# Fourteen gate tiles of a hybrid encoder block: full products, or seven block products to a pair of tiles

## The chip, the core and the metric

The kernel runs on one core of a Trainium2 chip. A core has TensorE (PE, matrix products; its weight loads are listed apart as PEld), VectorE (DVE), ScalarE (ACT), GpSimdE (POOL) and SyncE (SP), which here only issues transfers between DRAM and SBUF, the on-chip memory. PE writes to PSUM, eight banks of 128 x 512 float32. The engines run side by side, each through its own instructions in order; semaphores tie them together. The metric is the device time of one execution in microseconds (us); the kernel before takes 1192.48 us, the median of three runs (1191.15 to 1193.78).

## The reference

One layer on x of 1024 positions x 1024 channels, all float32:

```
xn = RMSNorm(x) * g
u, z_a, v, b, c, z_b, g_a, g_b = split(xn @ W_in)          # eight units of 1024 columns
y  = D*u + S5 scan forward + S5 scan backward              # 64 groups of 16 channels, state 64
y  = gelu(y);  y = y * sigmoid(y @ w_glu);  y_a = y * silu(z_a)
y_b = b * conv3(c * v) * silu(z_b)
merged = sigmoid(g_a) * (y_a @ w_branch_a) + sigmoid(g_b) * (y_b @ w_branch_b)
out = RMSNorm(x + merged @ w_out) * final_g
```

## The kernel before

**Layout.** Channels stand on the 128 partitions, positions along the free axis. A tile is 128 channels x 1024 positions, so 1024 channels are K = 8 tiles. Every float32 operand of a product is split in two: `hi` (the value cast to fp32r, by ACT, L808 or L115) and `lo` (the rest, by DVE, L809 or L116). One output tile of a product is 48 matmuls of 128x128 weights with 512 moving columns: 8 input tiles x 3 (hi·hi, hi·lo, lo·hi) x 2 halves of the positions (`matmuls`, L125 to L138).

**Order of the work.** After the norm and the first four tiles of u come 52 output tiles of W_in, one after the other (`projections`, the list `items`, L774 to L786): four of u, 32 for the convolution branch, eight of z_a, eight of g_b (unit 7; `gb` takes the sigmoid and stores it to DRAM, `gbd`). Between them, placed by an estimate of PE's and DVE's time (`est`, `vec`), stands the S5 layer: `ssm`, run by `beside`. In this stretch the order on PE and DVE is the one the code is written in (`manual_schedule`); on ACT and SP, and on all engines afterwards, a scheduler sets it before the program runs. When `ssm` is through, its memory is given back, the pool `p2` takes it (L822), and the eight tiles of y_b are loaded from DRAM and split there (L823 to L831).

**Then** come four products with eight output tiles each: `ob` (y_b with w_branch_b; each tile times its gate `gbd` gives `m1`), `ga` (unit 6, the gate g_a; `sga` in SBUF), `glu` and `oa`; last `o`, the product with w_out, 17 groups of 24 matmuls. While `ob` and `ga` run, ACT and DVE work out gelu (`yt`, `yq`, `yg`, L873 to L887), tile by tile, from pieces that SP loads (`yt<-yd`, eight transfers to a tile).

**Buffers.** `t4` is a ring of five 128x1024 tiles for whatever is short-lived; weights have two buffers each for `wraw`, `whi` and `wlo`; PSUM has two double-bank tiles (`mm`) for output tiles and four single banks (`bg`) for the rest.

## Time and profile before

| | |
|---|---|
| median of the runs | 1192.48 us |
| the profiled execution, its own time | 1191.38 us |
| its span, first to last instruction | 1189.6 us |
| PE busy | 1157.0 us, 97% |
| DVE busy | 682.8 us, 57% |
| ACT busy | 422.6 us, 36% |
| mean granted TensorE clock | 0.997 of full speed |

The profiled execution lies 1.1 us under the median, and 1.8 us of its time lie outside the span. PE's matmuls overlap, so one matmul's duration (389 ns) is longer than the step from one to the next; the step is a stretch's time over its count. The same holds in part for DVE, whose next instruction starts a little before the one ahead has ended.

### The profile page before, as it was taken

Reading aid. Unit: us, or ns where it says so; the run is one execution under the profiler, and the core shown is the slowest. Engines: PE = TensorE matmul, PEld = TensorE weight load, DVE = VectorE, ACT = ScalarE, POOL = GpSimd, SP = SyncE. Lnnn points to the kernel's source line nnn. Section 1 sums busy time; section 2 is a strip of 40 time slices with the busy share of each in tenths; the row PEclk is TensorE's granted clock in tenths of the full one; section 3 lists DMA queues with packets and bytes.
Section 4 is the critical chain, followed back from the end, with each engine's and each line's share of the span. In section 5 each row is a group of like instructions: output and inputs, shape, how many; then the busy total and the mean of one; then the engine's idle time right before and its main releaser. Section 6 shows DMA issues by size and latency. Waiting matters only on the chain.

```text
span 1189.6 us, 14821 instructions
## 1 busy us (share of the span) xinstructions
PE 1157.0 (97%) x5926; PEld 960.2 (81%) x5926; DVE 682.8 (57%) x1081; ACT 422.6 (36%) x482; POOL 14.5 (1%) x59
## 2 busy tenths in 40 slices
PE   6999999998899999999999999999999999999997
PEld 4778888877788888888888888888888888887886
DVE  6854698884889869868853311323614235446234
ACT  6344742456215561451363311211414114124111
...
GB/s 283 74 149 284 245 180 70 65 117 194 108 71 63 154 143 71 69 97 118 81 137 208 164 141 166 135 36 76 137 54 36 106 106 67 40 53 270 14 36 106
DMA packets 157817, 140.53 MB, mean 118 GB/s; under 512 B 10892, under 2 KB 138036, under 8 KB 157620
## 3 DMA queue, kind: packets, MB, share of 16 engines
...
HBM read 106.00 MB, written 29.36 MB: 114 GB/s over the span
## 4 chain that ended last, share of the span: by engine, by line
PE 91%; DVE 3%; ACT 2%; issue 2%; DMA 1%; POOL 0%; POOLq 0%; SPq 0%; ACTq 0%; DVEq 0%
PE ps_p L132 46%; PE ps_glu L132 7%; PE ps_ga L132 7%; PE ps_ob L132 7%; PE o L952 7%; PE ps_oa L132 7%; PE xps_x L552 2%; PE ps_u L132 2%; PE yps_y L582 1%; PE yps_y L581 1%; PE yps_y L580 1%; PE kf_y L631 1%; DMA wor<-in_w_out_dram 0%; POOL r_x L145 0%; DMA x<-in_x_dram 0%
## 5 line engine op out<-in xcount | busy, mean ns | idle before, releaser
L132 PE MATMUL ps_p<-xnh,wh_p 128*128 128x512 f32 x832 | 260.6, 394 | 0.0
L132 PE MATMUL ps_p<-xnl,wh_p 128*128 128x512 f32 x832 | 256.6, 390 | 0.0
L132 PE MATMUL ps_p<-xnh,wl_p 128*128 128x512 f32 x832 | 256.3, 389 | 0.0
L132 PEld LDWEIGHTS ps_p<-xnl,wh_p 128*128 128x128 f32 x832 | 156.2, 188 | 33.0
L132 PEld LDWEIGHTS ps_p<-xnh,wl_p 128*128 128x128 f32 x832 | 156.2, 188 | 32.9
L132 PEld LDWEIGHTS ps_p<-xnh,wh_p 128*128 128x128 f32 x832 | 153.3, 188 | 32.6 <-issue 3.2
L115 ACT CAST wh_p<-wr_p 128x1024 fp32r<-128x1024 f32 x52 | 54.7, 1052 | 227.6 <-PE ps_p L132 151.1
L116 DVE TENSOR_TENSOR wl_p<-wr_p,wh_p 128x1024 fp32r<-128x1024 f32 x52 | 63.4, 1218 | 77.7 <-ACT wh_p L115 77.7
L668 DVE TENSOR_TENSOR SB<-SB,st 128x32 f32<-128x32 f32 (+2 forms) x232 | 98.7, 425 | 8.0
L664 DVE TENSOR_TENSOR st<-SB,ac 128x64 f32<-128x64 f32 (+2 forms) x116 | 80.0, 690 | 8.1 <-DMA ac<-acd 5.2
L952 PE MATMUL o<-wo,mh 128*128 128x512 f32 (+1 forms) x272 | 79.8, 377 | 0.8 <-ACT mh L808 0.8
L952 PEld LDWEIGHTS o<-wo,mh 128*128 128x128 f32 x272 | 50.0, 188 | 10.5 <-ACT mh L808 1.2
L952 PE MATMUL o<-wo,ml 128*128 128x512 f32 (+1 forms) x136 | 51.3, 377 | 0.3 <-DVE ml L809 0.3
L540 DVE TENSOR_TENSOR g_x<-bdt_x,pwt_x 128x1024 f32<-128x1024 f32 x16 | 19.6, 1223 | 45.9 <-DMA bdt_x<-bd 27.6
L555 ACT COPY SB<-xps_x 64x512 f32<-64x512 f32 x32 | 35.2, 1101 | 21.5 <-PE xps_x L552 21.1
L610 ACT COPY Sx_y<-SB 64x1016 f32<-64x1016 f32 x16 | 33.9, 2122 | 22.1 <-DVE SB L668 21.8
L552 PE MATMUL xps_x<-U_x,bdt_x 128*128 128x128 f32 x256 | 33.0, 285 | 8.4 <-DVE bdt_x L542 4.4
L116 DVE TENSOR_TENSOR wl_glu<-wr_glu,wh_glu 128x1024 fp32r<-128x1024 f32 x8 | 9.8, 1224 | 54.3 <-ACT wh_glu L115 54.3
L552 PEld LDWEIGHTS xps_x<-U_x,bdt_x 128*128 128x128 f32 x256 | 32.0, 200 | 10.4 <-issue 9.7
L862 DVE TENSOR_TENSOR m<-ps_ob,m 128x1024 f32<-128x1024 f32 x8 | 9.8, 1224 | 51.7 <-PE ps_ob L132 51.6
L132 PE MATMUL ps_ob<-ybl,wh_ob 128*128 128x512 f32 x128 | 39.4, 389 | 0.0
L132 PE MATMUL ps_ob<-ybh,wl_ob 128*128 128x512 f32 x128 | 39.4, 389 | 0.0
...
## 6 DMA issues: line engine op xcount, KB each, us to landing
...
```

Of the source, the lines that this page charges most:

```text
L115: S.copy(out=hi, in_=raw)
L116: V.tensor_tensor(out=lo, in0=raw, in1=hi.bitcast(F32), op=ALU.subtract)
L132: nc.tensor.matmul(out=ps[:, 512 * h:512 * h + 512], lhsT=l[:, k, :], rhs=r[k][:, 512 * h:512 * h + 512], start=(k == 0 and i == 0), stop= ...
L540: V.tensor_tensor(out=g_, in0=Wi, in1=er, op=ALU.mult)
L552: nc.tensor.matmul(out=xps[:, P * j:P * j + P], lhsT=Wi[:, j, ri, :], rhs=U[:, j, :], start=True, stop=True)
L555: S.copy(out=dst[0:NG], in_=x3[0:NG])
L580: nc.tensor.matmul(out=o, lhsT=b["Wl"][:, j, 0, :], rhs=b["Sx"][:, j, 0, :], start=True, stop=False)
L581: nc.tensor.matmul(out=o, lhsT=b["Wl"][:, j, 1, :], rhs=b["Sx"][:, j, 1, :], start=False, stop=False)
L610: S.copy(out=Sx[0:NG, :, :, 1:P], in_=zsrc[0:NG, :, :, 0:P - 1])
L664: V.tensor_tensor(out=t_[:, 0:n].rearrange("p b r s g -> p b r (s g)"), in0=bcast(z.rearrange("p b r g -> p b (r g)"), 2, 2), in1=bcast(ac ...
L668: V.tensor_tensor(out=o, in0=o, in1=t_[:, 0:n, :, s_], op=ALU.add)
L952: nc.tensor.matmul(out=ps[:, 0:n], lhsT=l[:, ts_], rhs=r, start=(k == 0 and i == 0), stop=(k == K - 1 and i == 2))
```

## The change

Fourteen of the sixteen gate tiles (six of g_b, eight of g_a) leave the list of full products. They are done by pairs. A pair has the weights a and b (1024 x 128 each), cut in an upper and a lower half of the input channels; the positions are cut in two halves too. The pair's result is then a 2x2 block product, which Strassen's scheme (in Winograd's form) does with seven block products of 12 matmuls instead of eight. It needs

- four sums of the input, once for all pairs: `s31` holds S3 and S1, `s24` holds S2 and S4, for k = 0 to 3, split in hi (`sh`) and lo (`sl`). They are made in `beside`, after the S5 layer and in its memory (pool `sx`);
- per pair, four differences of weights, `fT1` to `fT4`, their splits `hT`/`lT`, the split of b's lower half (`hB22`, `lB22`) and that of a (`ha`, `la`). `prep` does this in stages, one pair ahead;
- per pair, seven additions on DVE from PSUM (`plus`), one copy and four sigmoids on ACT; the two tiles go to DRAM, to `gbd` or the new `gad`.

So all gates stand ahead of `ob`. The product loop `ga` is gone; `oa` loads its gate from `gad`. The tiles 0 and 1 of y_b are split into halves of xn that no block product reads; tiles 2 to 7 are loaded and split after the gates, when `p2` is opened. Gelu works in place, stores its result to DRAM (`ygd`) and takes the order 4 to 7, 0 to 3, since the places of tiles 0 to 3 hold y_b until `ob` ends; `glu` sums in that order (`ks`) and loads `yg` back for its last multiplication. The rest of the kernel stands as it was; on PE every row up to the end of the S5 layer and four output tiles beyond it is the same.

The diff, cut to its core:

```diff
+    gad = [dtile(f"gad{i}", [P, D]) for i in range(K)]
+    ygd = [dtile(f"ygd{i}", [P, D]) for i in range(K)]
...
-    items += [(wcol(7, i), gb(i)) for i in range(K)]
+    items += [(wcol(7, i), gb(i)) for i in range(2)]
...
+                if n + 1 == len(items) and k:
+                    if k == 1:
+                        late["first"] = load_pair(0)
+                    elif 2 <= k <= 6:
+                        while "S" not in late:
+                            flush[0] = True
+                            push()
+                        prep(0, late["first"], k)
...
-        late["p2"] = p2 = ctx.enter_context(tc.tile_pool(name="p2", bufs=1))
-        for k in range(K):
+        late["st"] = gs = ExitStack()
+        sx = gs.enter_context(tc.tile_pool(name="sx", bufs=1))
+        late["sw"] = gs.enter_context(tc.tile_pool(name="sw", bufs=1))
+        late["S"] = {n: [] for n in "1234"}
+        for k in range(HK):
+            xs = []
+            for kk in (k, k + HK):
+                x_ = t4(f"xf{kk}")
+                V.tensor_tensor(out=x_, in0=xnh[kk].bitcast(F32), in1=xnl[kk].bitcast(F32), op=ALU.add)
+                vec(1.18)
+                xs.append(x_)
+            yield True
+            for names, ops in (("31", ((xs[0], 0, xs[0], 1, ALU.subtract), (xs[0], 1, xs[1], 1, ALU.add))),
+                               ("24", ((None, 1, xs[0], 0, ALU.subtract), (xs[1], 0, None, 0, ALU.subtract)))):
+                f_ = t4(f"s{names}_{k}")
+                for h, (l, lh, r, rh, op) in enumerate(ops):
+                    V.tensor_tensor(out=f_[:, half[h]], in0=(before if l is None else l)[:, half[lh]],
+                                    in1=(f_ if r is None else r)[:, half[rh]], op=op)
+                h_ = sx.tile([P, D], F32R, tag=f"h{names}_{k}", name=f"sh{names}_{k}")
+                l_ = sx.tile([P, D], F32R, tag=f"l{names}_{k}", name=f"sl{names}_{k}")
+                split(f_, h_, l_)
+                vec(2.6)
+                for h, n in enumerate(names):
+                    late["S"][n].append((h_[:, half[h]], l_[:, half[h]]))
...
+            hi = tuple(xnh[2 * k + h][:, half[1]] for h in range(2))
+            lo = tuple(xnl[2 * k + h][:, half[1]] for h in range(2))
+            for h in range(2):
+                split(yt[:, half[h]], hi[h], lo[h])
...
+    pairs7 = [(7, i) for i in range(2, K, 2)] + [(6, i) for i in range(0, K, 2)]
+
+    def load_pair(p):
+        u, i = pairs7[p]
+        w = {}
+        for n, q in (("a", i), ("b", i + 1)):
+            w[n] = wp.tile([P, K, P], F32, tag="wraw", name=f"wr_{n}{p}")
+            nc.sync.dma_start(out=w[n], in_=wcol(u, q).rearrange("(k p) e -> p k e", p=P))
+        return w
...
+    def two(p, w, name, src, bufs=1):
+        h_ = late["sw"].tile([P, HK, P], F32R, tag=f"h{name}", name=f"h{name}_{p}", bufs=bufs)
+        l_ = late["sw"].tile([P, HK, P], F32R, tag=f"l{name}", name=f"l{name}_{p}", bufs=bufs)
+        split(src, h_, l_)
+        vec(0.66)
+        w[name] = (h_, l_)
+    def diff(p, w, name, x_, y_):
+        f_ = late["sw"].tile([P, HK, P], F32, tag="f4" if name == "T4" else "tf", name=f"f{name}_{p}",
+                             bufs=1 if name == "T4" else 3)
+        V.tensor_tensor(out=f_, in0=x_, in1=y_, op=ALU.subtract)
+        vec(0.66)
+        w["f" + name] = f_
+    def prep(p, w, stage):
+        a, b = w["a"], w["b"]
+        if stage == 2:
+            diff(p, w, "T1", b[:, 0:HK], a[:, 0:HK])
+            diff(p, w, "T2", b[:, HK:K], w["fT1"])
+        elif stage == 3:
+            hi = wp.tile([P, K, P], F32R, tag="whi", name=f"ha_{p}")
+            lo = wp.tile([P, K, P], F32R, tag="wlo", name=f"la_{p}")
+            split(a, hi, lo)
+            vec(1.18)
+            w["B11"], w["B21"] = (hi[:, 0:HK], lo[:, 0:HK]), (hi[:, HK:K], lo[:, HK:K])
+            two(p, w, "T2", w["fT2"])
+        elif stage == 4:
+            two(p, w, "T1", w["fT1"])
+            diff(p, w, "T3", b[:, HK:K], b[:, 0:HK])
+        elif stage == 5:
+            two(p, w, "T3", w["fT3"])
+            diff(p, w, "T4", a[:, HK:K], w["fT2"])
+        elif stage == 6:
+            two(p, w, "B22", b[:, HK:K])
+        elif stage == 0:
+            two(p, w, "T4", w["fT4"])
+    def seven(p, w):
...
+        def prod(n, xs):
+            ps = bank(f"g{n}_{p}")
+            for k in range(HK):
+                for i, (l, r) in enumerate(((0, 0), (0, 1), (1, 0))):
+                    nc.tensor.matmul(out=ps, lhsT=w[n][l][:, k, :], rhs=xs[k][r],
+                                     start=k == 0 and i == 0, stop=k == HK - 1 and i == 2)
+            est["pe"] += 12 * 0.2266
+            return ps
+        def plus(out, ps, in_):
+            V.tensor_tensor(out=out, in0=ps, in1=in_, op=ALU.add)
+            vec(0.66)
+        def gate(q, h):
+            S.activation(out=at(q, h), in_=at(q, h), func=AF.Sigmoid)
+        g = prod("B11", A(0, 0))
+        yield 0
+        S.copy(out=at(0, 0), in_=g)
+        g = prod("T2", sx["2"])
+        yield 1
+        plus(at(0, 1), g, at(0, 0))
+        g = prod("T1", sx["1"])
+        yield 2
+        plus(at(1, 0), g, at(0, 1))
+        g = prod("T3", sx["3"])
+        yield 3
+        plus(at(1, 1), g, at(1, 0))
+        gate(1, 1)
+        plus(at(0, 1), g, at(0, 1))
+        g = prod("B21", A(HK, 0))
+        yield 4
+        plus(at(0, 0), g, at(0, 0))
+        gate(0, 0)
+        g = prod("B22", sx["4"])
+        yield 5
+        plus(at(1, 0), g, at(1, 0))
+        gate(1, 0)
+        g = prod("T4", A(HK, 1))
+        yield 6
+        plus(at(0, 1), g, at(0, 1))
+        gate(0, 1)
+        u, i = pairs7[p]
+        for q in range(2):
+            nc.sync.dma_start(out=(gbd if u == 7 else gad)[i + q], in_=o_[q])
+    def gates():
+        w = late["first"]
+        for p in range(len(pairs7)):
+            for n in seven(p, w):
+                if n == 0:
+                    prep(p, w, 0)
+                    nxt = load_pair(p + 1) if p + 1 < len(pairs7) else None
+                if nxt and n:
+                    prep(p + 1, nxt, n)
+                yield
+            w = nxt
...
+        for _ in gates():
+            pass
+    late["st"].close()
...
+    p2 = ctx.enter_context(tc.tile_pool(name="p2", bufs=1))
+    for k in range(2, K):
+        yt = t4(f"ybt{k}")
+        nc.sync.dma_start(out=yt, in_=ybd[k])
+        h_, l_ = slot(p2, "B0", k, F32R, "ybh"), slot(p2, "B1", k, F32R, "ybl")
+        split(yt, h_, l_)
...
-    sga = []
-    for i in range(K):
-        ps = product(wcol(6, i), xnh, xnl, f"ga{i}")
-        s_ = slot(p2, "B0", i, F32, "sga")
-        S.activation(out=s_, in_=ps, func=AF.Sigmoid)
-        sga.append(s_)
-    yg, ygh, ygl = [], [], []
-    for k in range(K):
+    ygh, ygl = [None] * K, [None] * K
+    ks = [4, 5, 6, 7, 0, 1, 2, 3]
+    for k in ks:
...
-        y_ = slot(p2, "B1", k, F32, "yg")
-        V.tensor_tensor(out=y_, in0=yt, in1=q, op=ALU.mult)
-        yg.append(y_)
-    for k in range(K):
-        h_, l_ = slot(xnp, "A0", k, F32R, "ygh"), slot(xnp, "A1", k, F32R, "ygl")
-        split(yg[k], h_, l_)
-        ygh.append(h_)
-        ygl.append(l_)
+        V.tensor_tensor(out=yt, in0=yt, in1=q, op=ALU.mult)
+        nc.sync.dma_start(out=ygd[k], in_=yt)
+        ygh[k], ygl[k] = slot(xnp, "A0", k, F32R, "ygh"), slot(xnp, "A1", k, F32R, "ygl")
+        split(yt, ygh[k], ygl[k])
...
-        ps = product(w_glu[0][:, P * i:P * i + P], ygh, ygl, f"glu{i}")
+        ps = product(w_glu[0][:, P * i:P * i + P], ygh, ygl, f"glu{i}", ks=ks)
         zt = t4(f"zt{i}")
         nc.sync.dma_start(out=zt, in_=zsd[i])
+        y_ = slot(p2, "B1", i, F32, "yg")
+        nc.sync.dma_start(out=y_, in_=ygd[i])
         sg = t4(f"sgl{i}")
         S.activation(out=sg, in_=ps, func=AF.Sigmoid)
-        V.tensor_tensor(out=zt, in0=zt, in1=yg[i], op=ALU.mult)
-        V.tensor_tensor(out=yg[i], in0=zt, in1=sg, op=ALU.mult)
+        V.tensor_tensor(out=zt, in0=zt, in1=y_, op=ALU.mult)
+        V.tensor_tensor(out=y_, in0=zt, in1=sg, op=ALU.mult)
+        yg.append(y_)
...
+        nc.sync.dma_start(out=t_, in_=gad[i])
-        V.tensor_tensor(out=t_, in0=ps, in1=sga[i], op=ALU.mult)
+        V.tensor_tensor(out=t_, in0=ps, in1=t_, op=ALU.mult)
```

How the order moves, at three places. First DVE, from the end of the S5 layer to the first gate pair. `ks_y` is its last step, `ybl` the lo of a y_b tile, `wl_p` that of a weight, `sga` a z_a tile. Before:

```order
L564 SCALAR_TENSOR_TENSOR ks_y15_5269<-mask_131,Dk_130,ks_y15_5269 128x16
L566 TENSOR_TENSOR ks_y15_5269<-kf_y15_5251,ks_y15_5269 128x16
L809 TENSOR_TENSOR ybl0_5350<-ybt0_5347,ybh0_5349 128x1024
L770 TENSOR_TENSOR sga5_5360<-ps_p41_5216,sga5_5360 128x1024
L116 TENSOR_TENSOR wl_p43_5373<-wr_p43_5370,wh_p43_5372 128x1024
L809 TENSOR_TENSOR ybl1_5391<-ybt1_5388,ybh1_5390 128x1024
L809 TENSOR_TENSOR ybl2_5409<-ybt2_5406,ybh2_5408 128x1024
```

Now, the last twelve rows ahead of the moment at which the second block product can end:

```order
L899 TENSOR_TENSOR fT1_0_5634<-wr_b0_5626,wr_a0_5624 128x512
L899 TENSOR_TENSOR fT2_0_5636<-wr_b0_5626,fT1_0_5634 128x512
L819 TENSOR_TENSOR la_0_5645<-wr_a0_5624,ha_0_5644 128x1024
L819 TENSOR_TENSOR lT2_0_5649<-fT2_0_5636,hT2_0_5648 128x512
L819 TENSOR_TENSOR lT1_0_5659<-fT1_0_5634,hT1_0_5658 128x512
L899 TENSOR_TENSOR fT3_0_5662<-wr_b0_5626 128x512
L819 TENSOR_TENSOR lT3_0_5671<-fT3_0_5662,hT3_0_5670 128x512
L899 TENSOR_TENSOR fT4_0_5674<-wr_a0_5624,fT2_0_5636 128x512
L819 TENSOR_TENSOR lB22_0_5683<-wr_b0_5626,hB22_0_5682 128x512
L856 TENSOR_TENSOR s24_3_5692<-s31_3_5611,xf3_5591 128x512
L856 TENSOR_TENSOR s24_3_5692<-xf7_5593,s24_3_5692 128x512
L819 TENSOR_TENSOR sl24_3_5696<-s24_3_5692,sh24_3_5695 128x1024
```

Where eight splits stood, there are now eight additions over a whole tile, sixteen over half a tile, eight splits, and the preparation of the first pair; the last input sum, `s24_3`, stands behind that whole preparation.

Second SP, from the last gate pair to `ob`. `gad` and `gbd` stores are gates, `wr_ob` weights, `ybt` tiles of y_b, `m1` the gates read back. Before:

```order
L783 DMA gbd6_117<-sgb6_5927 128x1024
L112 DMA wr_ob2_6092<-in_w_branch_b_dram 128x8x128
L861 DMA m16_6379<-gbd6_117 128x1024
L877 DMA yt0_6896<-yd0_83 128x1x128 x3
L783 DMA gbd7_118<-sgb7_5972 128x1024
L112 DMA wr_ob3_6150<-in_w_branch_b_dram 128x8x128
```

Now:

```order
L1019 DMA ybt2_6689<-ybd2_93 128x1024
L1019 DMA ybt3_6695<-ybd3_94 128x1024
L1019 DMA ybt4_6701<-ybd4_95 128x1024
L114 DMA wr_ob3_6899<-in_w_branch_b_dram 128x8x128
L977 DMA gad7_126<-go6_1_6573 128x1024
L1028 DMA m10_6780<-gbd0_111 128x1024
L977 DMA gad6_125<-go6_0_6572 128x1024
L1019 DMA ybt5_6707<-ybd5_96 128x1024
L1019 DMA ybt6_6713<-ybd6_97 128x1024
L1019 DMA ybt7_6719<-ybd7_98 128x1024
```

Six loads of y_b have moved here, three of them behind the stores of the last gate pair.

Third DVE, from `ob` to what follows it. `m1` takes an `ob` tile out of PSUM, `yq` and `yt` are gelu, `ygl` the lo of its result, `wl` the lo of a weight. Before, around the last `ob` tile:

```order
L862 TENSOR_TENSOR m16_6379<-ps_ob6_6330,m16_6379 128x1024
L116 TENSOR_TENSOR wl_ga0_6443<-wr_ga0_6440,wh_ga0_6442 128x1024
L886 TENSOR_TENSOR yg0_6910<-yt0_6896,yq0_6905 128x1024
L886 TENSOR_TENSOR yg1_6926<-yt1_6912,yq1_6921 128x1024
L882 TENSOR_SCALAR yq2_6937<-yq2_6937 128x1024
L883 TENSOR_TENSOR yq2_6937<-yq2_6937,yt2_6928 128x1024
L886 TENSOR_TENSOR yg2_6942<-yt2_6928,yq2_6937 128x1024
L882 TENSOR_SCALAR yq3_6953<-yq3_6953 128x1024
L862 TENSOR_TENSOR m17_6437<-ps_ob7_6388,m17_6437 128x1024
```

Now:

```order
L1029 TENSOR_TENSOR m16_7128<-ps_ob6_7079,m16_7128 128x1024
L1047 TENSOR_TENSOR yt2_7309<-yt2_7309,yq2_7318 128x1024
L819 TENSOR_TENSOR ygl0_7286<-yt0_7269,ygh0_7285 128x1024
L819 TENSOR_TENSOR ygl1_7306<-yt1_7289,ygh1_7305 128x1024
L819 TENSOR_TENSOR ygl2_7326<-yt2_7309,ygh2_7325 128x1024
L1044 TENSOR_SCALAR yq3_7338<-yq3_7338 128x1024
L118 TENSOR_TENSOR wl_glu0_7352<-wr_glu0_7349,wh_glu0_7351 128x1024
L1045 TENSOR_TENSOR yq3_7338<-yq3_7338,yt3_7329 128x1024
L1060 TENSOR_TENSOR zt0_7404<-zt0_7404,yg0_7406 128x1024
L1047 TENSOR_TENSOR yt3_7329<-yt3_7329,yq3_7338 128x1024
L1029 TENSOR_TENSOR m17_7186<-ps_ob7_7137,m17_7186 128x1024
L819 TENSOR_TENSOR ygl3_7346<-yt3_7329,ygh3_7345 128x1024
```

At the last `ob` tile gelu was at its fourth tile of eight before; now it is at its eighth (tile 3), and the lo of `glu`'s first weight stands behind gelu's steps.

## Rows read from the trace of the kernel before

**Rows 1.** The page, part 1: busy time, share and instructions of each engine

```profile
PE 1157.0 (97%) x5926; PEld 960.2 (81%) x5926; DVE 682.8 (57%) x1081; ACT 422.6 (36%) x482; POOL 14.5 (1%) x59
```

**Rows 2.** The page, part 4: shares of the chain that ended last

```profile
PE 91%; DVE 3%; ACT 2%; issue 2%; DMA 1%; POOL 0%; POOLq 0%; SPq 0%; ACTq 0%; DVEq 0%
```

**Rows 3.** That chain in order of time, from 630 us: start, duration, what

```profile
636.23 108.84 PE ps_p L132 x480
745.07 87.04 PE ps_ob L132 x384
832.11 87.04 PE ps_ga L132 x384
```

**Rows 4.** Timeline of PE in product o: start, duration, instruction, count

```profile
1093.52 0.39 PE L952 MATMUL o<-wo,ml 128*128 128x512 f32 x1
1093.75 0.62 PE L952 MATMUL o<-wo,mh 128*128 128x512 f32 x2
```

**Rows 5.** Timeline of DVE, 618 to 647 us; in brackets the idle time ahead

```profile
620.28 0.69 DVE L618 TENSOR_TENSOR W_y<-W_y,gt_y 128x512 f32<-128x512 f32 x1
620.89 0.69 DVE L616 TENSOR_TENSOR W_y<-ce_y 128x512 f32<-128x512 f32 x1
...
626.10 0.17 DVE L566 TENSOR_TENSOR ks_y<-kf_y,ks_y 128x16 f32<-128x16 f32 x1
643.09 1.22 DVE L809 TENSOR_TENSOR ybl<-ybt,ybh 128x1024 fp32r<-128x1024 f32 x1 [16.82 <-ACT ybh L808]
644.24 1.22 DVE L770 TENSOR_TENSOR sga<-ps_p,sga 128x1024 f32<-128x1024 f32 x1
```

**Rows 6.** Timeline of ACT, 640 to 664 us

```profile
642.01 3.90 ACT L808 CAST ybh<-ybt 128x1024 fp32r<-128x1024 f32 x4 [5.11 <-DMA yd<-ys_y]
...
658.57 1.02 ACT L769 ACTIVATE sga<-ps_p 128x1024 f32<-128x1024 f32 x1
...
661.75 1.06 ACT L808 CAST ybh<-ybt 128x1024 fp32r<-128x1024 f32 x1 [0.16 <-DMA ybt<-ybd]
```

**Rows 7.** Timeline of SP's queue at three moments: issues of 512 KB transfers

```profile
655.48 0.32 SPq L825 DMA_DIRECT2D ybt<-ybd  x1
...
681.41 0.32 SPq L783 DMA_DIRECT2D gbd<-sgb  x1
...
684.51 0.32 SPq L861 DMA_DIRECT2D m<-gbd  x1
```

**Rows 8.** Table of stretches: length, busy time by engine, granted clock, DMA share, GB/s

```profile
280.00:290.00 10.00, 7.37 (x58) 6.93 (x57) 3.74 (x4) 5.28 (x7) 0.21 (x2) 1.00 0.68 173
...
297.00:305.00 8.00, 4.23 (x20) 4.12 (x21) 7.44 (x8) 2.25 (x3) 0.00 (x0) 0.79 0.46 118
...
745.00:832.00 87.00, 87.00 (x386) 72.03 (x385) 26.88 (x24) 15.54 (x16) 0.00 (x0) 1.00 0.28 84
832.00:919.00 87.00, 87.00 (x386) 72.03 (x385) 34.87 (x32) 32.16 (x33) 0.00 (x0) 1.00 0.26 78
```

**Rows 9.** Timeline of PE, 284 to 304 us: two waits of PE

```profile
288.85 2.02 PE L552 MATMUL xps_x<-U_x,bdt_x 128*128 128x128 f32 x16 [2.63 <-issue]
...
300.77 3.62 PE L552 MATMUL xps_x<-U_x,bdt_x 128*128 128x128 f32 x16 [4.41 <-DVE bdt_x L542]
```

**Rows 10.** Groups by line, whole run: count, busy us, mean ns, idle before

```profile
L808 ACT CAST wo<-wor 128x512 fp32r<-128x512 f32 x16 | 9.3, 619 | 15.7 <-DMA wor<-in_w_out_dram 12.2 <-PE ps_oa L132 3.5
...
L881 ACT ACTIVATE yq<-yt 128x1024 f32<-128x1024 f32 x8 | 8.5, 1058 | 11.8 <-DMA yt<-yd 8.6 <-DVE yg L886 2.9 <-ACT yq L884 0.3
...
L882 DVE TENSOR_SCALAR yq<-yq 128x1024 f32<-128x1024 f32 x8 | 5.5, 693 | 11.2 <-ACT yq L881 11.1
...
L883 DVE TENSOR_TENSOR yq<-yq,yt 128x1024 f32<-128x1024 f32 x8 | 9.8, 1225 | 0.2
```

**Rows 11.** By tile, yd: issues of the loads of gelu's input, ns least/median/most

```profile
L877 SPq DMA_DIRECT2D yt<-yd x64: 574/574/627, 739.2 to 854.0; - x64
```

More of the change, by code (lines that the diff above doesn't have):

```diff
@@ L117, in load_w, with product, matmuls @@
         return hi, lo
-    def product(w, rhi, rlo, name, by_half=False, w_pair=None):
+    def product(w, rhi, rlo, name, by_half=False, w_pair=None, ks=tuple(range(K))):
         whi, wlo = w_pair or load_w(w, name)
         ps = mm_tile(f"ps_{name}")
-        matmuls(ps, (whi, wlo), rhi, rlo, range(K), by_half)
+        matmuls(ps, (whi, wlo), rhi, rlo, ks, by_half, ks[0], ks[-1])
         return ps
-    def matmuls(ps, w, rhi, rlo, ks, by_half=False):
+    def matmuls(ps, w, rhi, rlo, ks, by_half=False, first=0, last=K - 1):
         pairs = ((w[0], rhi), (w[0], rlo), (w[1], rhi))
@@ L134, in matmuls @@
                 lhsT=l[:, k, :],
-                rhs=r[k][:, 512 * h:512 * h + 512],
-                start=(k == 0 and i == 0),
-                stop=(k == K - 1 and i == 2),
+                rhs=r[k][h] if isinstance(r[k], tuple) else r[k][:, 512 * h:512 * h + 512],
+                start=(k == first and i == 0),
+                stop=(k == last and i == 2),
             )
@@ L812, in block_kernel @@
     ybh, ybl = [], []
+    late = {}
+    HK = K // 2
+    half = (slice(0, 512), slice(512, D))
     def beside():
@@ L821, in beside @@
         tabs.close()
-        late["p2"] = p2 = ctx.enter_context(tc.tile_pool(name="p2", bufs=1))
-        for k in range(K):
+        late["st"] = gs = ExitStack()
[22 more added lines that the diff above has]
+                    late["S"][n].append((h_[:, half[h]], l_[:, half[h]]))
+                before = f_
+                yield True
@@ L824, in beside @@
+        for k in range(2):
             yt = t4(f"ybt{k}")
             nc.sync.dma_start(out=yt, in_=ybd[k])
-            h_, l_ = slot(p2, "B0", k, F32R, "ybh"), slot(p2, "B1", k, F32R, "ybl")
-            split(yt, h_, l_)
-            vec(3.0)
-            ybh.append(h_)
-            ybl.append(l_)
-            yield True
-    late = {}
+            hi = tuple(xnh[2 * k + h][:, half[1]] for h in range(2))
[3 more added lines that the diff above has]
+                vec(0.66)
+            ybh.append(hi)
+            ybl.append(lo)
+            yield True
@@ new lines, in seven @@
+    def seven(p, w):
+        sx = late["S"]
+        A = lambda o, h: [(xnh[o + k][:, half[h]], xnl[o + k][:, half[h]]) for k in range(HK)]
+        o_ = [t4(f"go{p}_{q}") for q in range(2)]
+        at = lambda q, h: o_[q][:, half[h]]
+        def prod(n, xs):
[8 more added lines that the diff above has]
+            V.tensor_tensor(out=out, in0=ps, in1=in_, op=ALU.add)
+            vec(0.66)
+        def gate(q, h):
[29 more added lines that the diff above has]
+            nc.sync.dma_start(out=(gbd if u == 7 else gad)[i + q], in_=o_[q])
@@ L853, in block_kernel @@
         push()
-    p2 = late["p2"]
+        for _ in gates():
[7 more added lines that the diff above has]
+        split(yt, h_, l_)
+        ybh.append(h_)
+        ybl.append(l_)
     m1 = []
@@ L884, in block_kernel @@
         S.activation(out=q, in_=q, func=AF.Sigmoid, scale=2.0 * math.sqrt(2.0 / math.pi))
[L885 to L892 removed]
+        V.tensor_tensor(out=yt, in0=yt, in1=q, op=ALU.mult)
+        nc.sync.dma_start(out=ygd[k], in_=yt)
+        ygh[k], ygl[k] = slot(xnp, "A0", k, F32R, "ygh"), slot(xnp, "A1", k, F32R, "ygl")
+        split(yt, ygh[k], ygl[k])
+    yg = []
     for i in range(K):
[L894 removed]
+        ps = product(w_glu[0][:, P * i:P * i + P], ygh, ygl, f"glu{i}", ks=ks)
         zt = t4(f"zt{i}")
         nc.sync.dma_start(out=zt, in_=zsd[i])
+        y_ = slot(p2, "B1", i, F32, "yg")
+        nc.sync.dma_start(out=y_, in_=ygd[i])
         sg = t4(f"sgl{i}")
         S.activation(out=sg, in_=ps, func=AF.Sigmoid)
[L899 to L900 removed]
+        V.tensor_tensor(out=zt, in0=zt, in1=y_, op=ALU.mult)
+        V.tensor_tensor(out=y_, in0=zt, in1=sg, op=ALU.mult)
+        yg.append(y_)
     yah, yal = [], []
```

## The prediction

> **What bounds the kernel now.** I read the page's busy times first: PE is at work for 1157.0 of 1189.6 us, with 5926 matmuls [rows 1]. Then the chain that ended last: 91% of it is PE [rows 2]. Its last third is PE without a break: from 636.23 us on, 480 matmuls of the projections take 108.84 us, and `ob` and `ga` 384 each in 87.04 us [rows 3]. That is 87.04 / 384 = 0.2267 us to a step of 512 columns, at full granted clock in the table of stretches [rows 8]. In that stretch DVE is busy for 26.88 of 87 us under `ob` and 34.87 under `ga`, ACT for 15.54 and 32.16 [rows 8]. So a matmul taken away there is worth its whole step, as long as DVE, ACT and SP bring the operands in time. All that the change adds lies on those three.
>
> **What goes from PE.** Fourteen tiles of 48 matmuls are 672; seven pairs of 7 x 12 are 588. 84 x 0.2267 = 19.0 us leave the path. Two things could spoil the step of those that stay: a block product changes its weights at two matmuls of three instead of at one in three, and writes twelve times running to one bank. In `o` both are so: groups of 24 go to one bank, and between `ml` and `mh`, which are different weights, the step is 1093.75 - 1093.52 = 0.23 us [rows 4]. I take 0.2267. The loop `ga` is only moved, so nothing else leaves PE.
>
> **The gate loop itself.** To a pair PE has 84 x 0.2267 = 19.0 us. DVE has four differences, five narrow splits and seven additions, 16 narrow (128x512) operations of 0.69 [rows 5] and one wide split of 1.22: 12.3 us. ACT has one wide cast (1.06, like any wide pass) and ten narrow ones (0.62): 7.3 us [rows 10]. A block product needs the bank of the fourth before it, so DVE may be 3 x 2.7 = 8.2 us late with an addition, less its 0.69. The next pair's weights are issued a pair ahead; their differences stand in DVE's queue before the addition for T1, which then waits with them. Cost taken: 0. What it costs without that cover is rival D.
>
> **The way in.** On PE the first block product comes four tiles after the S5 layer: 636.23 + 192 x 0.2267 = 679.8. The second, T2, needs the last input sum `s24_3`: its hi after 21 matmuls, at 684.5, its lo one matmul later, at 684.8. DVE must get there. Before, it stood idle from 626.3 to 643.09, since the memory of the S5 layer was free only when its last store had landed, at 642.01 [rows 5, 6]; the new hi tiles take the same memory, so I start the count there. From the first lo at 643.09 to the last, DVE's queue holds 19 wide operations (eight splits, six sums, four for the z_a tiles and their weights, one of the first pair), a step of 644.24 - 643.09 = 1.15 each [rows 5]: 21.9 us. It holds 22 narrow ones, between the step of 0.61 and the duration of 0.69 [rows 5], 0.65: 14.3 us. And seven times it waits for the cast of a sum it has just made, about 643.09 - 642.01 = 1.1 with the signal [rows 5, 6]: 7.7 us. 643.1 + 43.9 = 687.0, so PE waits 687.0 - 684.8 = 2.2, and some tenths for the narrow casts: 2.5 us. From below: should the memory come free early, DVE is still held by the last z_a tile, whose sigmoid ends at 658.57 + 1.02 = 659.6 [rows 6]; behind that stand nine wide, sixteen narrow and four casts, 10.4 + 10.4 + 4.4, which ends at 684.8: no wait. From above: 0.69 and 1.22 for every operation give 2.2 us more, 4.7. A wait here delays `plus` and the y_b splits behind it too, but those have the four banks for cover.
>
> **The way out.** At the end of the last block product, call it 0, `ob` has tiles 0 and 1 of y_b and, split one by one, 2 to 4: cast 1.06, lo 1.15 behind it, against 6 x 0.2267 = 1.36 of PE a tile, so these keep ahead. Tile 5 is loaded only after the last gate's store: addition 0.69, a cast that stands ahead on ACT 1.06, sigmoid 0.62, so its load is issued at about 2.2. Alone, a 512 KB transfer is through in 684.51 - 681.41 = 3.1 us; queued behind others it took from 655.48 to 661.75, 6.3 us [rows 6, 7]. With its cast that is 6.4 to 9.6, and PE's order has 35 matmuls, 7.9 us, before it asks. So 0 to 1.7 us of wait, and up to 3 with tiles 6 and 7 behind it. I take 1.0.
>
> The Trainium skill, SBUF — State Buffer, section "The DMA setup-cost knee", gives a transfer 2 us and its bytes at 436 GB/s; by that estimate 512 KB take 3.2 us, which agrees with the 3.1 and not with the 6.3. By the page tile 5 would be there in time, this wait 0, and the gain of the sum below 16.0 instead of 15.0 us. I keep the rows, since two loads and two stores share the queues there.
>
> **Gelu under `ob` alone.** It had 174 us (`ob` and `ga`) and now has 87. One tile on DVE is 0.69 + 3 x 1.22 = 4.4 us (a scaling, two products, the split's lo) [rows 10], beside `ob`'s own two wide operations, 2.4: 6.8 of 10.9 us per `ob` tile. ACT: 3 x 1.06 + 1.06 of 10.9. SP: 64 issues of 0.574 [rows 11] are 36.7 us. In SP's order the first tile's loads stand behind `ob`'s fifth weight, the last of them behind the sixth, and these two wait for DVE's work on `ob`'s first and second tile; so the chain of gelu tiles (3 x 1.06 + 4.4, nearly serial: 7.6 us each) starts some 28 us in. Followed through, wl_glu0 is ready about 2 us before `ob` ends, and tile 3, the last, about 4 us after its end, where `glu`, which sums 4 to 7 first, asks 7 x 1.36 = 9.5 us after. Between 0 and, should each tile slip by half a us, 5 us. I take 0.5, near the side that the counts reach.
>
> **Sum.** 19.0 - 2.5 - 1.0 - 0.5 = 15.0 us. The profiled execution's 1191.4 becomes 1176.4; it lay 1.1 under the median of the runs, so the forecast is 1192.5 - 15.0 = 1177.5. The 32 more transfers of 512 KB, a busy share of 0.26 to 0.28 before [rows 8], cost nothing of their own. In `oa` the gate is loaded well ahead of its use.
>
> **Rivals.** A change under 0.2%, 2.4 us, can't be told from none here.
>
> A, all of it comes: the three waits are hidden, 1192.5 - 19.0 = 1173.5. For it: PE runs 457 us to the end with hardly a pause, and DVE's idle 16.8 us [rows 5] lie just ahead of the new work. Against it: the casts between each sum and its lo, which no idle time shortens.
>
> B, the waits are at their upper ends: 4.7 + 3 + 2, and a long one costs the clock too. PE kept full clock past a wait of 2.63 us, but in the stretch with one of 4.41 it is 0.79 on average, that is in part at 1.2 GHz, and the sixteen matmuls behind it took 3.62 us instead of 2.02 [rows 8, 9], 1.6 more. 19.0 - 11.3 = 7.7: 1184.8. The Trainium skill, TensorE: Matmul & The Clock Gate, section "HAM oscillation", says that a gap in PE's work lets the clock fall and the next matmuls start slow; the trace agrees, with that 0.79.
>
> C, slower: gelu becomes a convoy. SP's loads of a gelu tile stand behind a weight that waits for DVE's split, which waits for an `ob` tile, and the store of gelu's result waits for DVE in the same queue. If the loop closes only once per `ob` tile, the eighth gelu tile ends at 28 + 8 x 10.9 = 115 instead of 28 + 8 x 8 = 92 (7.6 and the signals), and `glu` waits 115 - 97.5 = 17.5 us at tile 3, and 1.6 for the clock. With 3.5 from the other places that is 22.6 against 19.0: 1196.1. It decides from 28 + 8 t with t = 10.4 us a tile. Against it: 7.6 us of serial work, and in the order no gelu tile waits for an `ob` tile later than the one it follows.
>
> D, no change: in the gate loop weights land so late that an addition is over 7.5 us behind. If one block product of 2.7 us stands still at each of the six changes of pair, 16.3 us go, and 15.0 becomes -1.3: 1193.8. Against it: 1 MB in and 1 MB out per 19 us is about the rate of the stretch before [rows 8], and a landing would have to take some 12 us.
>
> **How the numbers follow.** Forecast 0.58, its own range 1174.5 to 1181. A 0.17, B 0.12, C 0.08, D 0.05. Faster by over 0.2% (under 1190.1): the forecast, A and nearly all of B, 0.86. Within: D and the rest of B, 0.05. Slower: C and a worse D, 0.09. The range takes in A and B: 1172.5 to 1186.
>
> **What would show it.** PE's matmuls 84 fewer at a step of 0.2267 in the gate stretch, 588 in 133.3 us. A wait of PE at T2 of the first pair, released by DVE's `sl` or ACT's `sh`, 0 to 4.7 us, and DVE without idle time from 643 to there but for the casts. A wait in the first `ob` tile, at tiles 5 to 7, released by ACT's `ybh` or DVE's `ybl`. No wait of PE on `plus` or on a weight from the second pair on. `glu` starting within 1 us of `ob`'s end. Wrong would be: a step over 0.23 us in the gates, PE waiting in every pair, or a wait in `glu` at its last input tiles.

## The result, and the profile after

The changed kernel takes 1179.2 us, the median of four runs (1177.95 to 1183.82), against 1192.1 for the kernel before: a ratio of 0.9897, 95% interval 0.9867 to 0.9927. The forecast was 1177.5. The profiled execution is the longest of the four, 1183.82. In two later comparisons the ratio was 0.9878 (0.9861 to 0.9895) and 0.9870 (0.9847 to 0.9892).

The page's first part, which answers to [rows 1]: 84 matmuls fewer, and less time on PE.

```profile
PE 1144.2 (97%) x5842; PEld 948.1 (80%) x5842; DVE 773.6 (65%) x1220; ACT 452.1 (38%) x541; POOL 14.5 (1%) x59
```

The chain that ended last, after the change, from 627 us on, answers to [rows 3]. Of the seven pairs the first and the last are shown.

```profile
627.95 5.66 PE ps_p L134 x24
...
639.66 4.16 DMA yd<-ys_y
643.92 1.06 ACT sh L818
645.01 1.23 DVE sl L819
...
687.44 1.05 ACT sh L818
688.51 1.24 DVE sl L819
689.79 7.80 PE gT L937 x26
697.59 5.44 PE gB L937 x24
...
708.47 8.16 PE gT L937 x36
716.63 5.44 PE gB L937 x24
...
811.83 5.45 PE gB L937 x24
817.31 0.70 DVE go L943
818.04 0.64 ACT go L947
818.69 3.31 DMA gad<-go
822.10 5.55 DMA ybt<-ybd
827.67 1.05 ACT ybh L818
828.77 79.40 PE ps_ob L134 x349
908.17 87.04 PE ps_glu L134 x384
...
1089.92 83.82 PE o L1115 x384
```

From 697.59 to 716.63, one pair, it is 19.04 us: 84 x 0.2267, without a wait. The chain leaves PE only twice between the S5 layer and the end of `glu`. The first time is from 639 to 690: it goes through the landing of the S5 layer's last store (`yd`, at 643.82) and then along DVE's queue, with a cast on ACT ahead of each lo, to the lo of the last input sum. The second is from 817 to 829, for tile 5 of y_b. These are the "way in" and the "way out". `glu` follows `ob` without a break.

The timeline of PE at the way in (start, duration, instruction, count; in brackets the idle time ahead and who ended it):

```profile
686.90 0.39 PE L937 MATMUL gT<-sh,lT 128*128 128x512 f32 x1
688.53 0.50 PE L937 MATMUL gT<-sh,hT 128*128 128x512 f32 x1 [1.25 <-ACT sh L818]
689.79 0.51 PE L937 MATMUL gT<-sl,hT 128*128 128x512 f32 x1 [0.76 <-DVE sl L819]
690.14 0.39 PE L937 MATMUL gT<-sh,lT 128*128 128x512 f32 x1
...
692.10 0.63 PE L937 MATMUL gT<-sh,lT 128*128 128x512 f32 x1
692.52 0.63 PE L937 MATMUL gT<-sh,hT 128*128 128x512 f32 x1
```

Two waits, 1.25 + 0.76 us, at the hi and the lo of `s24_3`, as the prediction said. But from 690.82 to 694.23 the matmuls start 0.43 us apart instead of 0.23: eight of them at the lower clock level, 1.2 GHz. The table of stretches shows the same (length, busy time of PE, PEld, DVE, ACT, POOL, then granted clock, DMA share, GB/s):

```profile
682.00:701.00 19.00, 16.99 (x67) 13.36 (x66) 13.32 (x21) 8.27 (x12) 0.00 (x0) 0.91 0.41 139
...
720.00:740.00 20.00, 20.00 (x90) 16.57 (x89) 13.03 (x21) 7.95 (x13) 0.00 (x0) 1.00 0.32 106
```

In the loop itself, the second row, DVE is busy for 13.03 of 20 us, 12.4 to a pair, and ACT for 7.95; PE never stops.

One execution says little about the parts that the change leaves alone, so the stretches are compared over all profiles. A stretch begins where the last y product of the S5 layer ends (start plus duration of its last row). It goes to the start of the first matmul of `ob`, and to the start of `glu`'s row in the chain, which lies 0.16 us behind the start of `glu`'s first matmul. The last two columns are PE's idle time in the first pair and the chain's row of `o`. The changed kernel's first two rows:

```profile
638.58 0.39 PE L584 MATMUL yps_y<-U_y,toe_y 128*128 128x128 f32 x2
...
819.83 0.62 PE L134 MATMUL ps_ob<-xnh,wh_ob 128*128 128x512 f32 x2
```

| profile | last y product ends | from there to `ob` | to `glu` | idle in first pair | `o` |
|---|---|---|---|---|---|
| before | 636.24 | | 282.91 | | 82.21 |
| before2 | 640.40 | | 282.91 | | 82.23 |
| changed kernel | 638.97 | 180.86 | 269.20 | 2.01 | 83.82 |
| again (same kernel) | 636.11 | 181.42 | 269.53 | 2.58 | 83.81 |
| again2 (same kernel) | 638.75 | 179.50 | 268.13 | 2.26 | 82.22 |
| order | 639.87 | 177.91 | 266.24 | 0.94 | 83.72 |
| both | 636.85 | 177.67 | 266.80 | 0.69 | 82.23 |
| head | 639.66 | 176.67 | 265.66 | 0 | 82.21 |
| best | 639.44 | 176.67 | 264.71 | 0 | 82.22 |
| best2 | 636.94 | 176.68 | 265.00 | 0 | 82.22 |
| gelu1 (edited behind `ob`'s start) | 636.79 | 178.63 | | 1.41 | 83.82 |

By the step of 0.2267, with no waits, the 780 matmuls to `ob` take 176.8 us and the 1164 to `glu` 263.9. From start to start it is 176.67, as head and best show, since a matmul starts 0.16 us before the one ahead has ended. The change saves 13.4 to 14.8 us up to `glu`, where the forecast's terms gave 19.0 - 2.5 - 1.0 = 15.5.

### The profile page after: what moved, and what is told of

It reads as the page before. It is cut to its first block, busy times and chain, and to the rows that moved or that the text cites. A ratio compares the mean times of both kernels' runs of the same rounds, so it can differ in the third digit from the quotient of the medians.

```text
span 1182.1 us, 14984 instructions
## 1 busy us (share of the span) xinstructions
PE 1144.2 (97%) x5842; PEld 948.1 (80%) x5842; DVE 773.6 (65%) x1220; ACT 452.1 (38%) x541; POOL 14.5 (1%) x59
## 4 chain that ended last, share of the span: by engine, by line
PE 83%; DVE 6%; DMA 4%; ACT 3%; issue 2%; SPq 1%; POOL 0%; POOLq 0%; ACTq 0%; DVEq 0%
PE ps_p L134 35%; PE ps_glu L134 7%; PE o L1115 7%; PE ps_oa L134 7%; PE ps_ob L134 7%; PE gT L937 6%; PE gB L937 5%; PE xps_x L554 2%; PE ps_u L134 2%; PE yps_y L584 1%; PE yps_y L583 1%; PE yps_y L582 1%; DVE s L856 1%; DVE sl L819 1%; ACT sh L818 1%
## 5 line engine op out<-in xcount | busy, mean ns | idle before, releaser
L134 PE MATMUL ps_p<-xnh,wh_p 128*128 128x512 f32 x736 | 231.5, 396 | 0.0
L134 PE MATMUL ps_p<-xnl,wh_p 128*128 128x512 f32 x736 | 227.5, 390 | 0.0
L134 PE MATMUL ps_p<-xnh,wl_p 128*128 128x512 f32 x736 | 227.0, 390 | 0.0
L134 PEld LDWEIGHTS ps_p<-xnl,wh_p 128*128 128x128 f32 x736 | 138.4, 188 | 29.4
L134 PEld LDWEIGHTS ps_p<-xnh,wl_p 128*128 128x128 f32 x736 | 138.4, 188 | 29.1
L134 PEld LDWEIGHTS ps_p<-xnh,wh_p 128*128 128x128 f32 x736 | 135.4, 188 | 28.9 <-issue 3.2
L943 DVE TENSOR_TENSOR go<-gT,go 128x512 f32<-128x512 f32 x35 | 23.5, 687 | 37.9 <-PE gT L937 17.9
L134 PE MATMUL ps_oa<-yal,wh_oa 128*128 128x512 f32 x128 | 39.5, 390 | 0.0
L134 PE MATMUL ps_oa<-yah,wh_oa 128*128 128x512 f32 x128 | 39.4, 389 | 0.0
L134 PE MATMUL ps_glu<-ygh,wh_glu 128*128 128x512 f32 x128 | 39.4, 389 | 0.0
```

The lines of the kernel that those rows point to most:

```text
L134: nc.tensor.matmul(out=ps[:, 512 * h:512 * h + 512], lhsT=l[:, k, :], rhs=r[k][h] if isinstance(r[k], tuple) else r[k][:, 512 * h:512 * h ...
L943: V.tensor_tensor(out=out, in0=ps, in1=in_, op=ALU.add)
```

## The experiments

**again, again2, before2: what differs without any edit.** The first profile was 7.4 us over the forecast for it. Is that the change?

> The changed kernel as it is, once more. Theory: in its first profile 2.7 us were lost ahead of the last y product of the S5 layer (its group of 24 matmuls began at 627.95 instead of 625.21) and 1.6 us in `o`, in code that the change leaves alone, and that differs from one execution to the next. Then this profile shows that group nearer 625 than 628, or `o` nearer 82.2 than 83.8 us, and again a wait of 1.5 to 2.5 us at T2 of the first pair with 1 to 1.6 us lost to the clock behind it, and 0.3 to 1.3 us in the first `ob` tile; the median is 1177.5 to 1180. Rival: the change itself makes the S5 stretch and `o` slower (other places in memory, more traffic): the group begins at 628 again and `o` takes 83.8 again.

> The kernel before, for a second profile of it. Theory (the S5 stretch differs by some us from one execution to the next, whatever the kernel, by waits of the x products and the clock behind them): the last y product ends 0.5 to 4 us off the 636.2 of the first profile or the waits of the x products are divided otherwise; and the 480 matmuls behind it and `ob` take 108.8 and 87.0 us again. Rival (the changed kernel makes the S5 stretch slower): 636.2 within 0.3 us.

Measured: again 1179.91 us (1176.82 to 1181.65). Its last y product ends at 636.11, not at 638.97; `o` takes 83.81 again, as the rival had it, with a wait of 1.54 us ahead of it; T2 waits 2.58 us, just over what was expected, and the clock falls behind it. The kernel before, profiled a second time (one run, 1196.56 us), is 4.2 us later at the same place; its chain from there on:

```profile
640.40 108.83 PE ps_p L132 x480
...
923.31 87.04 PE ps_glu L132 x384
```

So 636 or 640 at the end of the S5 layer is an execution's own, whatever the kernel, and from there to the end of `glu` the kernel before repeats to 0.01 us. `o` is slow after the change in two profiles of three, and 82.22 in again2, so its 1.6 us do not belong to every execution of the changed kernel: they come when the clock falls behind the wait at its start. The two profiles of the kernel before show no such `o`; two are too few to say that it has none.

> The changed kernel once more, on the same chip as the kernel named best. Theory: 180.5 to 181.5 us from the last y product to `ob`, 88 from there to `glu`; time as before, about 15 us under the kernel before.

Measured: 1178.31 us (1178.12 to 1180.18), 179.50 us to `ob`, 88.5 from there to `glu`'s first matmul. PE's two waits at T2:

```profile
688.56 0.49 PE L937 MATMUL gT<-sh,hT 128*128 128x512 f32 x1 [1.49 <-ACT sh L818]
689.82 0.50 PE L937 MATMUL gT<-sl,hT 128*128 128x512 f32 x1 [0.77 <-DVE sl L819]
```

They are longer than in the first profile, yet the clock stays at 1.00 behind them, and the stretch is 1.4 us shorter for it. The expectation of 180.5 to 181.5 took the clock's fall for certain and missed. Two runs below are edited only behind this place, so they are two more profiles of it: eight waits 1.40 + 0.77 us and gelu1 as follows, and in both the clock stays at 1.00.

```profile
685.76 0.50 PE L937 MATMUL gT<-sh,hT 128*128 128x512 f32 x1 [0.65 <-ACT sh L818]
687.02 0.50 PE L937 MATMUL gT<-sl,hT 128*128 128x512 f32 x1 [0.76 <-DVE sl L819]
```

So the clock fell at T2 in two profiles of five.

**eight: is the loop bound by PE?**

```diff
+        prod("B21", A(HK, 0))
         g = prod("B21", A(HK, 0))
```

> The changed kernel with the product B21 done twice in each pair (a second time into another bank, its first result unused): 84 matmuls more, eight block products a pair. Theory (the gate loop is bound by PE, and a matmul there is worth its step of 0.2267 us): 19.0 us slower than the changed kernel, 1198.2. Rival (PE waits in the loop for DVE or a bank, so that added matmuls fill waits): under 15 us. Other rival (one product more holds a bank that an addition needs late, and PE waits for banks): over 21 us.

Measured: 1199.3 us (1195.48 to 1203.75), 19.4 over again on the same chip. The chain that ended last, from one pair to the next:

```profile
717.82 8.16 PE gB L937 x36
...
739.58 8.16 PE gB L937 x36
```

From 717.82 to 739.58 it is 21.76 us to a pair of 96 matmuls, 0.2267 each. The theory holds: a matmul there is worth its whole step, and no wait takes in the added ones.

**dve2, dve4: how much cover DVE has in the loop.** The lo of each narrow split is written twice more, or four times more:

```diff
         split(src, h_, l_)
+        for _ in range(2):    # dve4: range(4)
+            V.tensor_tensor(out=l_, in0=src, in1=h_.bitcast(F32), op=ALU.subtract)
```

> The changed kernel with the lo of each of the five narrow splits of a pair written three times instead of once: ten narrow operations more on DVE in a pair, 35 pairs of splits in all. DVE's work in a pair goes from 12.3 to about 18.6 us, just under PE's 19.0. Theory (DVE's work lies under PE's, with four banks of slack): PE waits at most 0.5 us in each of pairs 2 to 7, the gate stretch gets 0 to 4 us longer, all of it in the first two pairs, where DVE starts late. Rival D of the prediction (the loop stands still once per change of pair when DVE is late): 2.7 us at each change, 16 us longer.

> As the kernel before it with four more writings of each lo instead of two: twenty narrow operations more, DVE's work in a pair about 25 us, over PE's 19.0. Theory: from here DVE is the bound, each pair takes DVE's time, 24.5 to 26 us instead of 19.0, and the gate stretch gets 38 to 50 us longer. Rival (additions wait in DVE's queue behind the splits of the next pair for longer than the sum of its work says, or DVE still has idle time of its own): over 55 us, or under 30.

Measured: one profile each, 1192.62 and 1233.82 us; to `ob` 192.57 and 227.83. The same stretch of 20 us in dve2, then in dve4:

```profile
740.00:760.00 20.00, 19.65 (x86) 15.64 (x85) 17.98 (x28) 6.76 (x12) 0.00 (x0) 1.00 0.32 104
```

```profile
780.00:800.00 20.00, 15.76 (x67) 12.08 (x66) 19.45 (x30) 5.26 (x8) 0.00 (x0) 1.00 0.31 106
```

PE's waits in a pair of dve2, and in dve4 one of the four that come back from pair to pair:

```profile
729.16 0.47 PE L939 MATMUL gB<-xnh,ha 128*128 128x512 f32 x1 [0.16 <-ACT go L949]
...
732.41 0.47 PE L939 MATMUL gT<-sh,hT 128*128 128x512 f32 x1 [0.26 <-ACT hT L818]
```

```profile
732.64 0.50 PE L939 MATMUL gB<-xnh,ha 128*128 128x512 f32 x1 [1.01 <-DVE go L945]
...
759.31 0.50 PE L939 MATMUL gB<-xnh,ha 128*128 128x512 f32 x1 [0.95 <-DVE go L945]
...
785.84 0.50 PE L939 MATMUL gB<-xnh,ha 128*128 128x512 f32 x1 [0.99 <-DVE go L945]
```

In dve2 a pair takes 20.0 to 20.2 us instead of 19.04: 1.0 lost, of which 0.35 to 0.8 is idle time (at most 0.5 was expected), far from the 2.7 of rival D. Its stretch grew by 11.7 and not by 0 to 4: six pairs give 6, and 4.9 come from what the expectation overlooked, that the first pair's splits stand ahead of the last input sum, so that T2 waited 6.44 + 0.47 us. In dve4 a pair takes 25.7 to 26.7 us, a little over the 24.5 to 26 expected, and the stretch is 47.0 longer, within the 38 to 50 expected; DVE is busy for 19.45 of 20 and sets the pace. 36 narrow operations and a wide one, by their durations of 0.69 and 1.22, are 26.1 us; the 26 of dve2 are 19.2, just PE's time, which is why PE begins to wait there. So the changed loop, with 12.3, has some 6 us of DVE's time to spare in a pair.

**order: the way in.** In the first pair B21, which needs no input sum, is done second:

```diff
         S.copy(out=at(0, 0), in_=g)
+        g21 = prod("B21", A(HK, 0)) if p == 0 else None
         g = prod("T2", sx["2"])
...
         plus(at(1, 0), g, at(0, 1))
+        if p == 0:
+            plus(at(0, 0), g21, at(0, 0))
+            gate(0, 0)
         g = prod("T3", sx["3"])
...
-        g = prod("B21", A(HK, 0))
+        if p:
+            g = prod("B21", A(HK, 0))
```

> In the first pair alone the product B21, which uses no input sum, is done second instead of fifth, so that T2 is asked for 12 matmuls, 2.72 us, later. Theory (the last input sum is 2.0 us late, and the gap costs 1.5 us of clock behind it): PE does not wait at T2, or less than 0.3 us, the clock in 684 to 700 stays at 1.00, and the kernel gains 2 to 3.5 us, median about 1176.3. Rival 1: DVE is the bound of the head, and the wait only moves to T1 or T3 behind it: gain under 0.7 us. Rival 2: the clock falls there for another reason than the wait: wait gone, 1.5 us of slow matmuls still there, gain 2.0.

Measured: no wait at T2, the clock at 1.00, and 3.5 us less to `ob` than again. The median does not show it: 1179.44 us (1176.93 to 1181.34) against 1179.91. The profiled execution had its S5 layer 3.8 us later than again's, so parts outside the stretch can hide the gain at this number of runs. A new wait of 0.94 us is there, at B22; PE's row and DVE's:

```profile
697.96 0.50 PE L937 MATMUL gB<-sh,hB 128*128 128x512 f32 x1 [0.94 <-DVE go L943]
```

```profile
694.11 2.59 DVE L819 TENSOR_TENSOR xnl<-ybt,xnh 128x512 fp32r<-128x512 f32 x4 [3.67 <-PE gT L937]
```

DVE stood idle for 3.67 us until the four splits of y_b began. The chain puts that down to a load of y_b (`688.63 6.10 DMA ybt<-ybd`) and the cast behind it, though the row names PE: the addition that frees B21's bank is queued behind those splits.

**both: the way out, first try.** Beside the edit of order:

```diff
-        yt = t4(f"ybt{k}")
+        yt = slot(p2, "C", k, F32, "ybt") if k >= 5 else t4(f"ybt{k}")
```

> As the kernel with B21 second in the first pair, and beside it tiles 5 to 7 of y_b are loaded into memory of the m1 tiles, which is free at the end of the gates, and no longer into the buffers that the last two gate tiles hold until they are stored. Theory (tile 5 is late by its load behind the last gate store): the load of tile 5 is issued 1 to 2 us earlier, the wait of 0.8 us in the first `ob` tile goes to 0 to 0.3, and the kernel is 0.5 to 0.9 us faster than with the first edit alone. Rival: the three loads, all at once, take longer beside the gate stores (over 6.5 us instead of 5.6), and the wait stays 0.5 or more.

Measured: the wait in the first `ob` tile grew to 1.45 us, and the stretch to `glu` is 0.6 longer than order's. SP's queue, then the cast that PE waited for:

```profile
814.76 0.32 SPq L1025 DMA_DIRECT2D ybt<-ybd  x1
816.37 0.32 SPq L983 DMA_DIRECT2D gad<-go  x1
816.74 1.45 SPq L1025 DMA_DIRECT2D ybt<-ybd  x2
```

```profile
823.24 1.04 ACT L818 CAST ybh<-ybt 128x1024 fp32r<-128x1024 f32 x1 [2.86 <-DMA ybt<-ybd]
```

Only one load got ahead of the last store; the next two still stand behind it, and the one that PE waited for took 6.5 us to land: a wait of over 0.5, as the rival had it. The median, 1176.66 us (1175.78 to 1177.05), is 2.8 under order's all the same. In the two profiles the difference is the S5 layer (3.0 earlier) and `o` (1.5 shorter), not the edit, whose own stretch got longer; that the other runs differ by the same parts is not shown.

**head, best, best2: both ends.** head is order with the splits of y_b tiles 0 and 1 moved from ahead of the first pair's additions into the second pair; best also does tiles 2 and 3 within the last pair, in the halves of xn that its first product has freed:

```diff
+                if p == 1 and n in (0, 2):
+                    yb_load(n // 2)
+                if p == 1 and n in (4, 6):
+                    yb_split(n // 2 - 2, 1)
+                if p == len(pairs7) - 1 and n in (1, 2):    # best only
+                    yb_load(n + 1)
+                if p == len(pairs7) - 1 and n in (4, 5):    # best only
+                    yb_split(n - 2, 0)
...
-    for k in range(2, K):
+    for k in range(4, K):    # best only
```

> As the kernel with B21 second in the first pair, and the splits of y_b tiles 0 and 1 (two wide loads, four narrow casts and four narrow los) are moved from DVE's and ACT's queues ahead of the first pair's additions into the second pair. Theory (with B21 second, PE waited 0.94 us at B22 of the first pair, because DVE stood 3.67 us behind the y_b loads, with the addition that frees B21's bank queued behind): PE waits nowhere between the last y product and `ob`; from the end of the last y product to the first matmul of `ob` it takes 780 x 0.2267 = 176.8 us, against 180.9 of the changed kernel in its first profile. Rival: DVE is still late in the first pair from its own work, and a wait of 0.5 us or more stays at an addition of that pair. The median then lies 2.5 to 4.5 us under the changed kernel's, but the S5 stretch and `o` differ by up to 4 us from one execution to the next, so that the stretch decides, not the median.

> As the kernel named head, and beside it tiles 2 and 3 of y_b are loaded and split during the last pair, into the half tiles of xn that its first product has freed, so that only tile 7 is loaded behind the last gate store. Theory (the wait in the first `ob` tile is the load of tile 5 queued behind that store): no wait in `ob`; from the end of the last y product to the first matmul of `glu` it takes (780 + 384) x 0.2267 = 263.9 us, against 269.2 in the changed kernel's first profile. Rival: the two loads on SP ahead of the gate stores and the weights delay these, and a wait of 0.5 us or more appears in the last pair or at `ob`'s weights. Median about 1175 by the theory, where the changed kernel has 1179.5.

> The kernel named best (B21 second in the first pair, the splits of y_b tiles 0 and 1 in the second pair, of tiles 2 and 3 in the last) on the same chip as the changed kernel. Theory (the two ends of the gate stretch cost 4.8 us in the changed kernel's profiles, 2.0 to 2.6 in waits at T2, 2.0 in clock behind them, 0.3 to 0.5 net in `ob`): 176.7 us from the last y product to `ob` again, and a median 3.5 to 5 us under the changed kernel's. Rival (what is saved there is waited for later, in `o` or elsewhere): under 1.5 us.

Measured: head 1177.15 us (1173.62 to 1177.95), 176.67 to `ob`, no wait on the way in; in `ob` it waits 1.47. best 1176.77 (1174.26 to 1180.27) and best2 1176.49 (1174.57 to 1178.6): 176.7 again, and 0.3 to 0.5 us of idle time left in `ob`, where none was expected. The chain in best2 around the first pair:

```profile
680.50 5.44 PE gB L925 x24
685.94 8.16 PE gT L925 x36
694.10 2.72 PE gB L925 x12
...
901.94 87.04 PE ps_glu L134 x384
```

From the last y product to `glu` best and best2 save 18.2 and 17.9 us against the kernel before, of the 19.0 that left PE. Against the changed kernel on the same chip the median is 1.8 us lower (1176.49 to 1178.31), not the 3.5 to 5 expected; the profiles show 3.1 there, since in again2 the clock had not fallen. The ratios to the kernel before, 0.9855 (0.9831 to 0.9880) for best2 and 0.9870 (0.9847 to 0.9892) for again2, overlap: that best is faster than the kernel before is shown, that it is faster than the changed kernel is shown in its stretch, and not settled by the times.

**gelu1: the room under `ob`.** The lo of each gelu tile is written twice.

> The changed kernel with the lo of each gelu tile written twice, eight wide operations more on DVE under `ob`, 9.2 us. In the changed kernel's first profile the last gelu tile was split at 911.4 us and `glu` asked for it at 917.5, so it has 6.1 us of slack. Theory (the eight tiles follow each other nearly serially, 7.6 us a tile): the split of the last one ends up to 9.2 us later, and PE waits 2 to 3.5 us in the first `glu` tile. Rival (DVE's idle time between the steps of a tile takes up the added work): the split ends less than 6 us later and PE doesn't wait.

Measured, one profile, 1182.89 us; PE's waits in the first `glu` tile and the end of DVE's added work:

```profile
913.63 0.73 PE L134 MATMUL ps_glu<-ygl,wh_glu 128*128 128x512 f32 x2 [0.41 <-DVE ygl L1052]
...
917.04 0.72 PE L134 MATMUL ps_glu<-ygl,wh_glu 128*128 128x512 f32 x2 [1.52 <-DVE ygl L1052]
```

```profile
915.76 1.22 DVE L1052 TENSOR_TENSOR ygl<-yt,ygh 128x1024 fp32r<-128x1024 f32 x1
```

The last tile is ready 916.98 - 904.45 = 12.53 us after `glu`'s first matmul; in the changed kernel it was 910.15 + 1.23 - 908.01 = 3.37. That is 9.2 later for 9.2 us of work: the tiles are a serial chain, and nothing is taken up by idle time. PE waited 0.41 + 1.52 = 1.93, a little under the 2 to 3.5 expected.

## Why the prediction was right

**What goes from PE: right.** 84 matmuls fewer, 19.04 us to a pair, and eight confirms the price, 0.2267 us a matmul in the loop as elsewhere: neither more changes of weights nor twelve matmuls to one bank cost anything there.

**The gate loop, 0: right.** No wait on an addition or a weight from the second pair on. Work on DVE was 12.4 us to a pair for 12.3 worked out.

**The way in, 2.5: the place and the wait right, the term too small.** The idle time was 2.0 to 2.6 us in the changed kernel's three profiles, 2.17 in eight and 1.41 in gelu1. DVE took 44.7 us from its first lo to the last (645.01 to 689.75), the same in all five, for 43.9 worked out: too little by 0.8. But it began 6.0 us after the last y product, where the start taken from the kernel before, 643.09 - 636.23, lies 6.9 behind it. The two misses cancel, so that the idle time came out so near is in part luck. What differs between the five profiles is when the S5 layer's last store lands and the first lo begins: 5.4, 6.0, 6.2, 6.3 and 6.6 us after the last y product, with idle times of 1.41, 2.01, 2.17, 2.26 and 2.58.

The price was more than the idle time: against the 176.67 of head, the stretch lost 4.2, 4.8 and 2.8 us. The two waits cost 0.55 us beside the idle time (2.82 - 2.26 in again2, 1.96 - 1.41 in gelu1), since the matmul ahead of each wait takes 0.39 and 0.50 us instead of a step of 0.23, and the one after the second 0.35. In two profiles of five the clock fell behind them, 1.6 us more. The step that failed is the one that put both at nothing: the restarts were not counted, and the clock's price was kept for rival B, where it is 1.6 us too, because a wait of 2.63 us had cost nothing [rows 9]. The Trainium skill, TensorE: Matmul & The Clock Gate, section "HAM oscillation", lets the clock fall behind a gap in PE's work; here that came in two profiles of five and not in the other three.

**The way out, 1.0: the size right, the path in part another.** The load of tile 5 was issued 2.3 us after the gates' end (2.2 worked out) and took 5.55 us, between the 3.1 and 6.3 of [rows 6, 7]. But the sum had it wait for the last gate's store to be issued, and by the chain the landing of the store ahead of that one (818.69 + 3.31) released it. Both ended at about the same time: the last store was issued at 821.68 for 0.32 us. In again2 the landing ended last, and the load came 0.5 us after the store's issue. So the 2.2 is right in part by luck. PE was idle 0.6 to 1.1 us in the three profiles, 1.65 in gelu1 and 1.79 in eight, and `ob` took 88.0 to 88.5 in the three instead of 87.04. The estimate by the Trainium skill, SBUF — State Buffer, section "The DMA setup-cost knee", 3.2 us and no wait, did not hold beside other transfers.

**Gelu, 0.5: on the safe side.** No wait. The last tile was there 6.1 us before `glu` asked for it, for 5.5 counted; gelu1 shows the chain as serial as taken. By those 6.1 us PE would begin to wait only after some 6 us of added work, an estimate that fits its wait of 1.93 for 9.2; rival C did not come.

**The sum.** By the stretch 15.5 were forecast, and 13.4 to 14.8 came: the restarts and the clock on the way in are missing. The 0.5 set aside for gelu, which lies behind the stretch and was not needed, makes up for part of it in the forecast of 15.0; by the medians 12.9, 15.1 and 15.3 came. The distance of the first profile from the forecast, 7.4 us, is for the larger part not lost in every execution: 2.7 in the S5 layer (not in again), 1.6 in `o` and 1.6 by the clock at T2 (neither in again2).
